# Products of a weight group in another order: all on the upper halves first, then those on the lower halves

## The chip, the cores and the metric

One core of a Trainium2 chip runs the whole program. The metric is the device time of one execution in microseconds. The engines are named as the profile names them: PE is TensorE (its weight loads are PEld), ACT is ScalarE, DVE is VectorE, POOL is GpSimd, SP is SyncE, which issues most of the DMAs.

## What is computed

Two blocks on 256 tokens of width 2048, in float32. The first is a mixer (attention and a state-space scan side by side) and a layer of product-key experts; the second is a pooling layer and an attention layer with an index that selects keys. All have large projections:

```python
def first_block(x, ...):
    h = x
    for layer in range(DEPTH):                  # DEPTH = 1
        xn = rms_norm(h, attn_norm[layer])
        h = h + hybrid_mixer(xn, w_in[layer], ..., w_out[layer])
        hn = rms_norm(h, ffn_norm[layer])
        h = h + peer_ffn(hn, peer_query[layer], peer_sub_keys[layer], peer_down[layer], peer_up[layer])
    return h

def second_block(x, c, ...):
    cond = jax.nn.silu(c)
    for i in range(DEPTH_2):                    # DEPTH_2 = 2
        mod = cond @ mod_w[i] + mod_b[i]
        shift, scale, gate = jnp.split(mod, 3, axis=-1)
        h = rms_norm_2(x, norm_g[i]) * (1.0 + scale[:, None, :]) + shift[:, None, :]
        ...                                     # pool_branch, then dsa_branch
        x = x + gate[:, None, :] * out
    return rms_norm_2(x, final_g)
```

## The kernel before

A float32 matrix product is made of three products of halves. Both operands are split into an upper half (the value rounded to the type float32r) and a lower half (the rest), and `mm3` adds x-lower by w-upper (L169), x-upper by w-lower (L170) and x-upper by w-upper (L171) into one accumulator in PSUM. The activations `x` are the stationary operand (128 x 128), the weights the moving one (128 x 512).

Weights come in groups of 1 MB: 4 blocks of 128 rows by 512 columns, in one tile `wr` of a pool of three. `split_w` issues the load on SP (L154) and makes the halves in two steps of two blocks each, into pools of three tiles `wh` and `wl`:

```python
wh = self.whp.tile([128, 2, 512], F32R, tag="wh", name=self.nm("wh"))
nc.scalar.activation(wh, wr[:, s], AF.Copy)                                    # L159, ACT
wl = self.wlp.tile([128, 2, 512], F32R, tag="wl", name=self.nm("wl"))
nc.vector.tensor_tensor(wl, wr[:, s], wh.bitcast(F32), op=OP.subtract)         # L161, DVE
```

So a group has two tiles `wh` and two tiles `wl`, here called the first and the second upper and lower half. `wl` needs `wh`, and the tile `wr` is free for another load once both `wl` of it are made. A new `wh` or `wl` needs the slot of the third last one, whose products must have run.

`product` (called by `linear`) runs the groups of a projection for 256 tokens: for each of the 4 blocks k and each of the 2 token tiles t the three products of `mm3`, 24 in a group. `product2` does it for the expert layer, where 192 of the tokens go through dense products: three products for the first 128 tokens into one accumulator, and two into another (L219 and L220), whose stationary tile `xp` holds the upper and the lower half of 64 tokens side by side; 20 in a group. The last 64 tokens of that layer take gathered rows of the expert tables instead (`gathers`: POOL issues the gathers at L772, DVE multiplies a row at L780 and adds one at L795, 2.3 us each). Gate values of the experts are read back from DRAM into tiles `fm` and multiplied at L865. With `skew`, the last two groups of a layer are drawn so that the first token tile ends early.

After each group `step` lets waiting pieces of other work (transposes, attention, the scan, parts of the modulation `mod_w` at L1014) follow in the program. The order on each engine is then set by a scheduler: instructions have the priority of their place in the code, the load and the split of weights stand 1000 places ahead (`PRIO`), and the scheduler takes what its own estimate of times says is ready. On the chip each engine runs its list in that order.

Of the kernel before, what the change touches and what calls it, by code (L numbers as in the profile page):

```python
# [37 lines left out]
class Kern:  # L38
# [139 lines left out]
    def product(self, ps, groups, first=True, last=True, hook=None, skew=False):  # L178


        n = len(groups)
        held = []
        for gi, (src, i, xs) in enumerate(groups):
            if hook:
                hook(gi)
            hs, ls = self.split_w(src, i)
            held += [(x, h, l, first and gi == kk == 0, last and gi == n - 1 and kk == 3)
                     for kk, (x, h, l) in enumerate(zip(xs, hs, ls))]
            m = 2 if skew and gi == n - 2 else len(held)
            now, held = held[:m], held[m:]  # L190
            order = [(a, t) for a in now for t in range(2)]
            if skew and gi == n - 1:
                order.sort(key=lambda a: a[1])
            for ((xh, xl), h, l, st, sp), t in order:
                s = slice(t * 128, t * 128 + 128)
                self.mm3(ps[t], xh[:, s], xl[:, s], h, l, st, sp)
            self.step()

    def product2(self, ps, groups, skew=False):

        n = len(groups)
        held = []
        mm = self.nc.tensor.matmul
        for gi, (src, i, xs) in enumerate(groups):
            hs, ls = self.split_w(src, i)
            held += [(x, h, l, gi == kk == 0, gi == n - 1 and kk == 3)
                     for kk, (x, h, l) in enumerate(zip(xs, hs, ls))]
            m = 2 if skew and gi == n - 2 else len(held)  # L210
            now, held = held[:m], held[m:]
            order = [(a, t) for a in now for t in range(2)]
            if skew and gi == n - 1:
                order.sort(key=lambda a: a[1])
            for ((xh, xl, xp), h, l, st, sp), t in order:
                if t == 0:
                    self.mm3(ps[0], xh, xl, h, l, st, sp)
                else:
                    mm(ps[1], xp, h, start=st, stop=False)  # L219
                    mm(ps[1], xp, l, start=False, stop=sp)  # L220
            self.step()

    def step(self):


        self.posts = [g for g in self.posts if next(g, self) is not self]
        while self.seq:
            if next(self.seq[0], self) is not self:
                break
            self.seq.pop(0)  # L230
        if self.pump:
            self.credit += PUMP
            while self.credit >= 1:
                self.credit -= 1
                next(self.pump, None)
        self.bg_due += self.bg_rate
        while self.bg_due >= 1:
            self.bg_due -= 1
            self.bg(1)
# [1263 lines left out]
```

## Time and profile before

| | |
|---|---|
| median of 3 runs | 2774.44 us (2774.32 to 2775.48) |
| the profiled execution, in all | 2777.65 us |
| its span from the first to the last instruction | 2775.9 us |
| its mean granted clock of TensorE | 0.983 |
| busy: PE, DVE, ACT | 2642.5, 2244.1, 1394.2 us |
| DMA | 782.08 MB, 282 GB/s in the mean |

Busy time is that of one profiled execution, on one core. A product of 128x512 counts as busy for about 0.39 us, but the next one issues before it ends, so that a busy PE isn't yet one that issues as often as it can; how far apart two products stand is read from their starts in the timeline. "[0.67 <-DVE wl L161]" behind a row is the idle time of the engine ahead of it, and what ended it. The chain is followed back from the last instruction, at each step to what released it.

### The profile page before, as it was taken

To read this page: it belongs to the slowest core of one execution; us is meant where nothing else is said; L and a number is where in the kernel's file an instruction comes from. 1 tells how busy PE (TensorE), PEld (TensorE's weight loads), DVE (VectorE), ACT (ScalarE), POOL (GpSimd) and SP (SyncE) were. 2 spreads that over 40 slices of the span, in tenths; PEclk is the share of its full clock that TensorE was granted. 3 is DMA by queue.
4 is the path that set the end of the run, shared out by engine and by line. 5 is a ranking of instruction groups with operands and counts; after the bars stand their busy time and mean duration, and the time that the engine had idled before them with its cause. 6 is when DMAs were issued, how large, how long until landed. Compare 5 with 4: busy or idle time off the path is not lost.

```text
span 2775.9 us, 33244 instructions
## 1 busy us (share of the span) xinstructions
PE 2642.5 (95%) x12296; PEld 2142.0 (77%) x12296; DVE 2244.1 (81%) x3162; ACT 1394.2 (50%) x1881; POOL 271.3 (10%) x210
## 2 busy tenths in 40 slices
PE   8999999998998999999999899998999799999998
PEld 6787778877876777787877677777887687888886
DVE  6988886999997898768998789967779867765655
ACT  5547555554654444454544444444444444455543
POOL 1000000001112222102322212000000000000000
PEclk9999999999999999999999999999999899999999
DMA  7666675557999999869999999765788855655554
GB/s 291 261 224 227 259 261 203 195 202 265 382 374 398 358 372 373 320 238 334 406 366 374 353 363 357 291 224 219 277 304 324 310 201 193 226 208 187 182 194 170
DMA packets 135123, 782.08 MB, mean 282 GB/s; under 512 B 14000, under 2 KB 38736, under 8 KB 43760
## 3 DMA queue, kind: packets, MB, share of 16 engines
q1 hardware_dynamic: 113680, 639.81, 62.4%
q0 software_dynamic: 20752, 138.53, 12.8%
q8 instruction: 96, 1.57, 0.2%
q10 hardware_dynamic: 528, 1.61, 0.2%
q14 instruction: 67, 0.55, 0.1%
HBM read 759.11 MB, written 20.23 MB: 281 GB/s over the span
## 4 chain that ended last, share of the span: by engine, by line
PE 64%; DVE 14%; DMA 13%; issue 4%; ACT 3%; POOL 0%; ACTq 0%; DVEq 0%; POOLq 0%; SPq 0%
PE acc L170 16%; PE acc L171 16%; PE acc L169 16%; DVE wl L161 6%; PE acc L219 5%; PE acc L220 5%; DMA wr<-in_down 4%; DMA wr<-in_up 4%; ACT wh L159 2%; DMA wr<-in_mod_w 2%; DVE md L1014 1%; PE tr L267 1%; DVE gl L795 1%; DVE fm L780 1%; DMA wr<-in_pool_w_out 1%
## 5 line engine op out<-in xcount | busy, mean ns | idle before, releaser
L159 ACT ACTIVATE wh<-wr 128x1024 fp32r<-128x1024 f32 x944 | 991.4, 1058 | 1127.1 <-PE acc L171 380.7
L161 DVE TENSOR_TENSOR wl<-wr,wh 128x1024 fp32r<-128x1024 f32 x944 | 1140.5, 1220 | 408.2 <-ACT wh L159 398.9
L170 PE MATMUL acc<-wl,fm 128*128 128x512 f32 x1952 | 775.0, 397 | 29.5 <-DVE wl L161 28.7
L169 PE MATMUL acc<-wh,fm 128*128 128x512 f32 x1952 | 780.6, 402 | 16.4 <-ACT wh L159 14.4
L171 PE MATMUL acc<-wh,fm 128*128 128x512 f32 x1952 | 768.3, 394 | 0.0
L170 PEld LDWEIGHTS acc<-wl,fm 128*128 128x128 f32 x1952 | 370.5, 190 | 124.1 <-DVE wl L161 50.7
L169 PEld LDWEIGHTS acc<-wh,fm 128*128 128x128 f32 x1952 | 369.5, 190 | 95.5 <-ACT wh L159 18.8
L171 PEld LDWEIGHTS acc<-wh,fm 128*128 128x128 f32 x1952 | 370.1, 190 | 75.0
L170 PE MATMUL acc<-wl,gl 128*128 128x512 f32 x768 | 307.9, 401 | 18.6 <-DVE wl L161 18.6
L169 PE MATMUL acc<-wh,gl 128*128 128x512 f32 x768 | 305.2, 398 | 10.6 <-ACT wh L159 9.4
L171 PE MATMUL acc<-wh,gl 128*128 128x512 f32 x768 | 302.6, 394 | 0.0
L1014 DVE SCALAR_TENSOR_TENSOR md<-wr,c_c,md 128x1024 f32<-128x1024 f32 x180 | 230.4, 1280 | 35.4 <-DMA wr<-in_mod_w 33.4
L219 PE MATMUL acc<-wh,s 128*128 128x512 f32 x512 | 202.8, 396 | 0.0
L220 PE MATMUL acc<-wl,s 128*128 128x512 f32 x512 | 202.7, 396 | 0.0
L219 PE MATMUL acc<-wh,fm 128*128 128x512 f32 x512 | 202.2, 395 | 0.0
L220 PE MATMUL acc<-wl,fm 128*128 128x512 f32 x512 | 202.0, 395 | 0.0
L170 PEld LDWEIGHTS acc<-wl,gl 128*128 128x128 f32 x768 | 145.2, 189 | 63.9 <-DVE wl L161 31.8
L169 PEld LDWEIGHTS acc<-wh,gl 128*128 128x128 f32 x768 | 145.0, 189 | 46.0 <-ACT wh L159 12.2
L772 POOL DMA_INDIRECT fm<-in_up_rows,slot_rows x64 | 124.0, 1938 | 482.1 <-DVE gl L795 257.0
L171 PEld LDWEIGHTS acc<-wh,gl 128*128 128x128 f32 x768 | 145.5, 189 | 31.7 <-issue 1.0
L795 DVE SCALAR_TENSOR_TENSOR gl<-fm,slot_act,gl 128x2048 f32<-128x2048 f32 x63 | 147.7, 2344 | 6.1 <-DMA fm<-in_up_rows,slot_rows 6.1
L780 DVE SCALAR_TENSOR_TENSOR fm<-fm,gl 128x2048 f32<-128x2048 f32 x64 | 146.1, 2284 | 0.2 <-DMA fm<-in_down_rows,slot_rows 0.2
(416 smaller groups left out, 2377.6 us busy)
## 6 DMA issues: line engine op xcount, KB each, us to landing
wr<-in_down SPq DMA_DIRECT2D x128, 1024.0 KB, 8.6
wr<-in_up SPq DMA_DIRECT2D x128, 1024.0 KB, 8.1
wr<-in_mod_w SPq DMA_DIRECT2D x96, 1024.0 KB, 5.2
wr<-in_attn_w_in SPq DMA_DIRECT2D x72, 1024.0 KB, 4.8
wr<-in_w_in SPq DMA_DIRECT2D x44, 1024.0 KB, 5.2
wr<-in_pool_w_in SPq DMA_DIRECT2D x32, 1024.0 KB, 5.3
wr<-in_w_out SPq DMA_DIRECT2D x16, 1024.0 KB, 4.8
wr<-in_peer_query SPq DMA_DIRECT2D x16, 1024.0 KB, 4.7
```

What stands on the lines that cost most here:

```text
L159: nc.scalar.activation(wh, wr[:, s], AF.Copy)
L161: nc.vector.tensor_tensor(wl, wr[:, s], wh.bitcast(F32), op=OP.subtract)
L169: mm(ps, xl, wh, start=first, stop=False)
L170: mm(ps, xh, wl, start=False, stop=False)
L171: mm(ps, xh, wh, start=False, stop=last)
L219: mm(ps[1], xp, h, start=st, stop=False)
L220: mm(ps[1], xp, l, start=False, stop=sp)
L267: self.nc.tensor.transpose(p[:, j, t * 128:(t + 1) * 128], src(t, k + j), self.ident)
L772: nc.gpsimd.indirect_dma_start(rows[j], None, d[src], bass.IndirectOffsetOnAxis(ap=ei[:, j:j + 1], axis=0))
L780: nc.vector.scalar_tensor_tensor(r, r, 1.0, x2, op0=OP.mult, op1=OP.mult, accum_out=act[:, j - 2:j - 1])
L795: nc.vector.scalar_tensor_tensor(acc, r, c, acc, op0=OP.mult, op1=OP.add)
L1014: nc.vector.scalar_tensor_tensor(acc, w[:, j], cd[:, k:k + 1], acc, op0=OP.mult, op1=OP.add)
```

## The change

Inside a group the products are put into another order. `product` and `product2` no longer call `mm3` or the matmul for each block and token tile, but write what there is to do into a list `todo`; the new function `halves` runs first all products of the list that read an upper half of the weights, and then all that read a lower half. Where the last group of a layer is drawn by token tile (`skew`), it does so for each token tile by itself. `split_w`, the pools and the number of products stay as they were.

```diff
+            todo = []
             for ((xh, xl), h, l, st, sp), t in order:
                 s = slice(t * 128, t * 128 + 128)
-                self.mm3(ps[t], xh[:, s], xl[:, s], h, l, st, sp)
+                todo.append((t, st, sp, [(xl[:, s], h), (xh[:, s], h)], [(xh[:, s], l)]))
+            self.halves(ps, todo, skew and gi == n - 1)
             self.step()
...
+            todo = []
             for ((xh, xl, xp), h, l, st, sp), t in order:
                 if t == 0:
-                    self.mm3(ps[0], xh, xl, h, l, st, sp)
+                    todo.append((t, st, sp, [(xl, h), (xh, h)], [(xh, l)]))
                 else:
-                    mm(ps[1], xp, h, start=st, stop=False)
-                    mm(ps[1], xp, l, start=False, stop=sp)
+                    todo.append((t, st, sp, [(xp, h)], [(xp, l)]))
+            self.halves(ps, todo, skew and gi == n - 1)
             self.step()
+
+    def halves(self, ps, todo, by_t):
+
+
+        for part in ([[a for a in todo if a[0] == t] for t in range(2)] if by_t else [todo]):
+            ops = [(t, st and i == 0, False, x, w) for t, st, _, up, _ in part for i, (x, w) in enumerate(up)]
+            ops += [(t, False, sp, x, w) for t, _, sp, _, low in part for x, w in low]
+            for t, st, sp, x, w in ops:
+                self.nc.tensor.matmul(ps[t], x, w, start=st, stop=sp)
```

On PE, in a group of `product2` in the stretch with gathers (it starts at 1077.92 us in the timeline of before), the first five products before; `acc_1753` and `acc_1754` are the two accumulators, `wh_1762` and `wl_1763` the first halves of the group, `wh_1764` and `wl_1765` the second, `fm_685` to `fm_687` the activations:

```order
L169 MATMUL acc_1753_9037<-wh_1762_9074,fm_686_3650 128x512 [waits Activation_49]
L170 MATMUL acc_1753_9037<-wl_1763_9076,fm_685_3649 128x512 [waits DVE_49]
L171 MATMUL acc_1753_9037<-wh_1762_9074,fm_685_3649 128x512
L219 MATMUL acc_1754_9038<-wh_1762_9074,fm_687_3651 128x512
L220 MATMUL acc_1754_9038<-wl_1763_9076,fm_687_3651 128x512
```

The tenth to the fourteenth product of the same group, changed:

```order
L232 MATMUL acc_1753_9037<-wh_1764_9078,fm_686_3650 128x512
L232 MATMUL acc_1753_9037<-wh_1764_9078,fm_685_3649 128x512
L232 MATMUL acc_1754_9038<-wh_1764_9078,fm_687_3651 128x512
L232 MATMUL acc_1753_9037<-wl_1763_9076,fm_685_3649 128x512 [waits DVE_49]
L232 MATMUL acc_1754_9038<-wl_1763_9076,fm_687_3651 128x512
```

The first product on `wl_1763`, and with it the wait for DVE, moved from the second place of the group to the thirteenth, behind all twelve products on `wh_1762` and `wh_1764`.

On DVE at the same place before (L780 is the product of a gathered row, L161 makes the lower halves):

```order
L161 TENSOR_TENSOR wl_1763_9076<-wr_1761_9072,wh_1762_9074 128x1024 [waits DMAHW4_49,Activation_49]
L780 SCALAR_TENSOR_TENSOR fm_1891_9743,slot_act_5650<-fm_1891_9743,gl_680_3640 128x2048 [waits DMASW0_49]
L161 TENSOR_TENSOR wl_1765_9080<-wr_1761_9072,wh_1764_9078 128x1024 [waits PE_49,Activation_49]
L161 TENSOR_TENSOR wl_1768_9106<-wr_1766_9102,wh_1767_9104 128x1024 [waits DMAHW5_49,PE_49,Activation_49]
L780 SCALAR_TENSOR_TENSOR fm_1909_9825,slot_act_5650<-fm_1909_9825,gl_680_3640 128x2048 [waits DMASW1_49]
```

And changed (L791 is the line that was L780, L901 adds an accumulator to `h`, L905 another to a sum):

```order
L791 SCALAR_TENSOR_TENSOR fm_1891_9743,slot_act_5650<-fm_1891_9743,gl_680_3640 128x2048 [waits DMASW0_49]
L161 TENSOR_TENSOR wl_1759_9047<-wr_1755_9039,wh_1758_9045 128x1024 [waits PE_49,Activation_49]
L161 TENSOR_TENSOR wl_1763_9076<-wr_1761_9072,wh_1762_9074 128x1024 [waits DMAHW4_49,PE_49,Activation_49]
L901 TENSOR_TENSOR h_118<-h_118,acc_1737_8956 128x512
L161 TENSOR_TENSOR wl_1765_9080<-wr_1761_9072,wh_1764_9078 128x1024 [waits PE_49,Activation_49]
L161 TENSOR_TENSOR wl_1768_9106<-wr_1766_9102,wh_1767_9104 128x1024 [waits DMAHW5_49,PE_49,Activation_49]
L905 TENSOR_TENSOR gl_1581_8164<-gl_1581_8164,acc_1738_8957 128x512
L791 SCALAR_TENSOR_TENSOR fm_1909_9825,slot_act_5650<-fm_1909_9825,gl_680_3640 128x2048 [waits DMASW1_49]
```

The gathered row that stood between `wl_1763` and `wl_1765` now stands two lower halves earlier, and the making of `wl_1763` waits for PE too.

On PE in the first layer, ahead of a group of `product` (`wh_120` is its first upper half, `tr_131` a block of transposes for the convolution), before:

```order
L267 MATMUL tr_131_892<-ident_104,s2_107_748 128x128
L267 MATMUL tr_131_892<-ident_104,s2_108_749 128x128
L169 MATMUL acc_117_813<-wh_120_817,fm_5_127 128x512 [waits Activation_49]
L169 MATMUL acc_118_814<-wh_120_817,fm_5_127 128x512
L170 MATMUL acc_117_813<-wl_121_819,fm_4_126 128x512 [waits DVE_49]
L171 MATMUL acc_117_813<-wh_120_817,fm_4_126 128x512
```

And changed (L278 is the line that was L267):

```order
L278 MATMUL tr_130_885<-ident_104,s2_107_748 128x128 [waits Activation_49]
L278 MATMUL tr_131_892<-ident_104,s2_107_748 128x128 [waits PE_49]
L232 MATMUL acc_117_813<-wh_120_817,fm_5_127 128x512 [waits Activation_49]
L232 MATMUL acc_117_813<-wh_120_817,fm_4_126 128x512
L232 MATMUL acc_118_814<-wh_120_817,fm_5_127 128x512
L232 MATMUL acc_118_814<-wh_120_817,fm_4_126 128x512
```

Most of the transposes moved behind the group, and the group begins with products on `wh_120` alone.

## Rows read from the trace of the kernel before

**Rows 1.** The page: busy time by engine, and the chain by engine.

```profile
PE 2642.5 (95%) x12296; PEld 2142.0 (77%) x12296; DVE 2244.1 (81%) x3162; ACT 1394.2 (50%) x1881; POOL 271.3 (10%) x210
...
PE 64%; DVE 14%; DMA 13%; issue 4%; ACT 3%; POOL 0%; ACTq 0%; DVEq 0%; POOLq 0%; SPq 0%
```

**Rows 2.** Waits, who for whom: us in total, times, longest us.

```profile
DVE wl L161 <- ACT wh L159: 398.9, 334, 11.2
ACT wh L159 <- PE acc L171: 380.7, 240, 4.5
...
PEld acc L170 <- DVE wl L161: 82.4, 89, 7.4
...
PE acc L170 <- DVE wl L161: 47.2, 57, 7.0
...
PEld acc L169 <- ACT wh L159: 31.0, 23, 9.2
```

**Rows 3.** The page's groups: busy us, mean ns, idle before, releaser.

```profile
L159 ACT ACTIVATE wh<-wr 128x1024 fp32r<-128x1024 f32 x944 | 991.4, 1058 | 1127.1 <-PE acc L171 380.7
L161 DVE TENSOR_TENSOR wl<-wr,wh 128x1024 fp32r<-128x1024 f32 x944 | 1140.5, 1220 | 408.2 <-ACT wh L159 398.9
```

**Rows 4.** Timeline, 1076 to 1086 us: start us, us, what, idle before.

```profile
1077.71 1.23 DVE L161 TENSOR_TENSOR wl<-wr,wh 128x1024 fp32r<-128x1024 f32 x1 [1.97 <-ACT wh L159]
...
1077.92 0.40 PE L169 MATMUL acc<-wh,fm 128*128 128x512 f32 x1
1078.85 2.28 DVE L780 SCALAR_TENSOR_TENSOR fm<-fm,gl 128x2048 f32<-128x2048 f32 x1
...
1078.99 0.50 PE L170 MATMUL acc<-wl,fm 128*128 128x512 f32 x1 [0.67 <-DVE wl L161]
...
1080.24 0.39 PE L170 MATMUL acc<-wl,fm 128*128 128x512 f32 x1
...
1080.26 2.00 ACT L159 ACTIVATE wh<-wr 128x1024 fp32r<-128x1024 f32 x2 [1.64 <-DMA wr<-in_down]
1080.47 0.39 PE L171 MATMUL acc<-wh,fm 128*128 128x512 f32 x1
...
1080.69 0.39 PE L219 MATMUL acc<-wh,fm 128*128 128x512 f32 x1
...
1081.06 2.35 DVE L161 TENSOR_TENSOR wl<-wr,wh 128x1024 fp32r<-128x1024 f32 x2
1081.15 0.39 PE L169 MATMUL acc<-wh,fm 128*128 128x512 f32 x1
...
1082.34 0.50 PE L170 MATMUL acc<-wl,fm 128*128 128x512 f32 x1 [0.80 <-DVE wl L161]
...
1084.28 0.39 PE L220 MATMUL acc<-wl,fm 128*128 128x512 f32 x1
```

**Rows 5.** The chain in order of time, three pieces: start us, us, what.

```profile
50.35 0.79 PE acc L170
...
998.03 0.03 DVEq L161
...
2192.57 0.50 PE acc L170
```

**Rows 6.** Stretches: us, busy by engine (instructions), clock, DMA share, GB/s.

```profile
694.00:1180.00 486.00, 454.95 (x2268) 363.36 (x2267) 423.21 (x431) 240.91 (x297) 100.00 (x61) 0.99 0.95 368
...
1250.00:1800.00 550.00, 523.66 (x2273) 417.97 (x2272) 492.61 (x443) 262.55 (x294) 118.98 (x64) 0.98 0.93 356
```

**Rows 7.** Timeline of DVE and of PE, 886 to 906 us.

```profile
901.46 0.96 DVE L865 TENSOR_TENSOR gl<-gl,fm 128x768 f32<-128x768 f32 x1 [7.87 <-DMA fm<-gates]
...
903.61 0.79 PE L170 MATMUL acc<-wl,fm 128*128 128x512 f32 x1 [6.97 <-DVE wl L161]
```

**Rows 8.** The page's DMA issues: times, KB each, us to landing.

```profile
wr<-in_down SPq DMA_DIRECT2D x128, 1024.0 KB, 8.6
wr<-in_up SPq DMA_DIRECT2D x128, 1024.0 KB, 8.1
```

More of the change, by code (lines that the diff above doesn't have):

```diff
@@ L204, in product2 @@
         held = []
-        mm = self.nc.tensor.matmul
         for gi, (src, i, xs) in enumerate(groups):
```

## The prediction, before the changed kernel ran

> **What bounds the kernel now.** I read the page's chain and busy shares first. TensorE is busy 95% of the span, and 64% of the chain that ended last lies on it [rows 1]; VectorE has 14% of the chain, DMA 13%. So most of the time is plain products, and the order of products takes nothing from those: their number stays. What an order can change is the rest of the chain, where TensorE waits. The table of waits says for what: the line that reads a lower half (L170) waited for the lower half (`wl`) for 47.2 us in 57 waits on PE, and the load ahead of it for 82.4 us in 89 waits; the load of the line that reads an upper half (L169) waited for it 31.0 us in 23 [rows 2]. The load's figure is the truer one, since a product stays "busy" for 0.39 us while the next could follow after 0.23 us. So the late operand is mostly the lower half. That is natural: ScalarE makes `wh` in 1058 ns, and only then VectorE makes `wl` from it in 1220 ns [rows 3].
>
> The timeline of one group shows it [rows 4]. The upper half is there and L169 issues at 1077.92; `wl` runs from 1077.71 for 1.23 us, so L170 issues only at 1078.99. VectorE then works 2.28 us on a gathered row (L780), the second `wl` comes after that at 1081.06, and L170 issues at 1082.34 where L169 had at 1081.15. The group's last product issues at 1084.28.
>
> Such a wait costs the span only where the chain goes through it. I counted in the chain's pieces: 32 times it enters TensorE at L170 behind a `wl`, first at 50.35, last at 2192.57 [rows 5]. Of these 22 lie between 694 and 1800 us, the two stretches with gathers, where DMA share is 0.95 and 0.93 and VectorE is busy 423 of 486 and 493 of 550 us [rows 6]: three resources are close to full there. The other 10 lie outside.
>
> **The change part by part.** Nothing is removed or added: as many products, loads, splits and DMAs. In a group of 20 products (a `product2` group) TensorE now runs 12 on upper halves and then 8 on lower ones; in a `product` group 16 and then 8. Products issue 0.227 us apart: L170 at 1080.24, L171 at 1080.47, L219 at 1080.69 [rows 4].
>
> *When operands are needed.* The first lower half was needed by the second product of a group (or third, where the scheduler drew an upper one forward); now by the 13th or 17th. That is 11 x 0.227 = 2.5 us of cover in the short group, against a lag of about 1.2 us. The second lower half was needed by product 12 and is now by product 17: 1.1 us more. The second upper half is needed earlier, by product 7 instead of 11; ScalarE makes both halves back to back (x2 in 2.00 us at 1080.26 [rows 4]), so it is 1.0 us behind the first and needed 1.36 us behind: covered. In the group at 1077.92 I get: 12 products to 1080.64, four on the first lower half (ready at 1078.94) to 1081.55, then a wait for the second until about 1082.34 as before, and the last product at 1083.02 instead of 1084.28: 1.26 us gained, though both waits were not removed in full.
>
> *The gain.* 82.4 us / 89 waits = 0.93 us for one; 32 on the chain: 29.8 us. One of them is 7 us long: VectorE stood 7.87 us behind a DMA of gate values, L170 then waited 6.97 us [rows 7]; there only 2.5 us are covered, so 4.5 us come off: **25.3 us**. Bounds: from 0 (every wait comes back as a wait for `wh`) to 82.4 us (all of them were worth something). The waits beside the chain I price at nothing: behind them TensorE would only have waited for the next DMA, and that is what is late next.
>
> *When buffers come free.* An upper half's slot is free earlier: after product 6 instead of 10 (the first), after 12 instead of 20 (the second). ScalarE now waits for TensorE at this point, 380.7 us behind L171 alone, and VectorE for ScalarE, 398.9 us in 334 waits [rows 2]. A lower half's slot is free later: the first after product 16 instead of 10. Before, `wl` of the next group could start at 10 x 0.227 + 1.06 (ScalarE first) = 3.33 us into a group, now at 16 x 0.227 = 3.63: 0.30 us later. For the other half it was 20 x 0.227 + 1.06, now it is 20 x 0.227: 1.06 us earlier. The chain leaves TensorE for VectorE's queue at L161 14 times (one at 998.03 [rows 5]), all in the gather stretches: between 14 x 0.30 = 4.2 us lost and 14 x 1.06 = 14.8 us gained. I take 0, since VectorE at 87 to 90% busy has little room to start earlier. Behind that `wl` on VectorE stand gathered rows of 2.28 us, sums of products and the release of the weight's DMA slot; with both halves alternating, that release moves by the same few tenths, against the 8.6 us that a load takes to land [rows 8].
>
> *Moved steps.* The scheduler puts some transposes of the first layer a group earlier or later among the products. A group is 24 x 0.227 = 5.4 us; I bound the effect by plus or minus one group and take 0.
>
> *A rule that speaks against it.* The loads: 12296 products stand beside 12296 loads [rows 1], and L171, which reads the same stationary slice as L170 ahead of it, issues 0.23 us after it, as L219 does with another slice [rows 4]. So sharing is worth nothing here. The Trainium skill (TensorE: Matmul & The Clock Gate, Part 2, step by step) says that loads are separate so that one can serve many products; by that the old order, with two products in a row on one stationary slice, should hold an advantage that the new one drops. The trace disagrees, and no row here prices such an advantage; were there one, it would show as another spacing, which is the last rival below.
>
> Sum: 2775.9 - 25.3 = 2750.6 us against the profiled span. That execution took 2777.65 us in all; the runs' median is 2774.44, so **2749 us**.
>
> **The rivals.**
>
> *DMA stays the bound in the gather stretches* (0.18). At a share of 0.95 and 0.93 an earlier product only waits longer for the next weights: the waits change names, from `wl` to `wh`. For it: TensorE's own waits for `wh` exist already [rows 2]. Against it: the chain runs on TensorE for long pieces between the DMA pieces, and the share isn't 1. Then only the 10 entries outside count: 10 x 0.93 = 9.3 us, less up to 4.2 us at the exits: 2765 to 2769 us. About half of this lies within 0.2% (5.5 us, which is about what a measurement of this kernel can tell from no change).
>
> *More comes back* (0.13). If the earlier upper slots let the queue of DMA, ScalarE and VectorE close its gaps, the gather stretches could shrink until DMA is full: 0.05 x 486 + 0.07 x 550 = 63 us: 2712 us at most, some 2725 if half of it and the outer 10 come.
>
> *VectorE's queue is blocked* (0.08, slower). `wl` for the first half now waits directly for TensorE, later in the group, and all behind it on VectorE waits too: the gathered rows, and the adds that free accumulators. The place is the 256 `product2` groups (128 loads of down, 128 of up [rows 8]). Price: 0.30 us each, 77 us if all pay; half of them, less the forecast's gain, is 38 - 25 = 13 us slower: 2787 us. It decides from the point where VectorE has under 0.30 us to spare in a group: now it has (486 - 423) / 486 = 13% of 4.5 us, 0.6 us, and 10%, 0.5 us, so it should hold. The row in which VectorE stood behind a gate DMA [rows 7] shows that such a block does reach TensorE. The Trainium skill (TensorE: Matmul & The Clock Gate, Part 1, on the array's architecture) calls ScalarE's and VectorE's queues strictly first in, first out; that row agrees.
>
> *The products themselves space differently* (0.03). One nanosecond on each of 12296 is 12.3 us. Now the spacing is the same where the accumulator changes and where it doesn't (L171 to L219, L170 to L171 [rows 4]), so I expect none.
>
> That the change doesn't do what it says is excluded by the rows of its order: upper ones first, lower ones behind.
>
> **How the numbers follow.** Forecast 0.58 (2749), more 0.13 (2712 to 2735), DMA-bound 0.18 (2765 to 2769), VectorE blocked 0.08 (2774 to 2826), spacing 0.03. Faster by over 0.2%: 0.58 + 0.13 + 0.08 = 0.79; within: 0.11; slower: 0.10. The range runs from 2716, near full DMA in the gather stretches, to 2772, which takes in the DMA-bound case; outside are the blocked VectorE and the last of "more".
>
> **What would show it.** Right: in the table of waits the products' wait for `wl` falls from 47.2 us to under 15; the chain enters TensorE at an upper half; products still 0.227 us apart; gather stretches some 17 us shorter. DMA-bound: the wait for `wh` grows by what `wl` lost and those stretches keep their length. Blocked: VectorE's `wl` waits for PE by tens of microseconds and the gathers' rows come later. Wrong altogether: another spacing, or new waits at transposes over 10 us.

## The result, and the profile after

The changed kernel took **2787.74 us** (median of 13 runs, 2777.35 to 2812.78) against 2774.32 us (13 runs, 2768.41 to 2782.84) for the kernel before on the same chip: a ratio of **1.0059, interval 1.0037 to 1.0081**. It is slower by about 0.6%, where 2749 us and "faster" had been forecast; the time lies outside the range, on the other side. The profiled execution took 2782.33 us, near the low end of its runs, so its trace shows about 5 us of a difference of 13.

The page of after, busy time by engine and the groups of the two halves (columns as in [rows 3]), answers [rows 1, 3]:

```profile
PE 2631.4 (95%) x12296; PEld 2139.7 (77%) x12296; DVE 2234.3 (80%) x3162; ACT 1392.1 (50%) x1881; POOL 284.3 (10%) x210
...
L159 ACT ACTIVATE wh<-wr 128x1024 fp32r<-128x1024 f32 x944 | 986.7, 1058 | 1078.1 <-PE acc L232 524.1
L161 DVE TENSOR_TENSOR wl<-wr,wh 128x1024 fp32r<-128x1024 f32 x944 | 1124.2, 1220 | 424.5 <-PE acc L232 274.4
...
wr<-in_down SPq DMA_DIRECT2D x128, 1024.0 KB, 6.9
wr<-in_up SPq DMA_DIRECT2D x128, 1024.0 KB, 7.3
```

The number of instructions and the mean time of each are the same. What is new is at the end of the second line: before, VectorE's idle time ahead of a lower half was for ScalarE (398.9 us); now most of it is for TensorE. The waits of after, who for whom, total, times and longest in us (all products of a group now stand on line 232), answer [rows 2]:

```profile
ACT wh L159 <- PE acc L232: 524.1, 415, 6.7
...
DVE wl L161 <- PE acc L232: 274.4, 147, 4.4
...
ACT wh L159 <- DMA wr<-in_up: 178.0, 66, 9.6
...
ACT wh L159 <- DMA wr<-in_down: 147.2, 58, 7.0
DVE wl L161 <- ACT wh L159: 143.8, 105, 6.4
...
PE acc L232 <- ACT wh L159: 41.2, 24, 9.9
PE acc L232 <- DVE wl L161: 34.5, 32, 2.9
```

The same view of before has for these:

```profile
ACT wh L159 <- DMA wr<-in_up: 113.4, 45, 12.3
ACT wh L159 <- DMA wr<-in_down: 109.2, 36, 7.6
...
PE acc L169 <- ACT wh L159: 23.8, 13, 9.2
...
DVE wl L161 <- PE acc L219: 4.9, 3, 2.5
...
DVE wl L161 <- PE acc L220: 1.4, 1, 1.4
```

Three things are to be seen. VectorE's wait for TensorE to let a lower slot go went from 6.3 us (4.9 and 1.4) to 274.4 us. ScalarE waited 103 us longer for the weights of down and up to land, 325.2 against 222.6, although a load landed sooner after its issue (6.9 and 7.3 us, against 8.6 and 8.1 in [rows 8]): so it went out later, as seen from ScalarE, which is itself free earlier now. And TensorE won 12.7 us on lower halves and lost 17.4 us on upper ones. The stretches with gathers answer [rows 6] (busy by engine, clock, DMA share, GB/s):

```profile
694.00:1180.00 486.00, 451.82 (x2224) 362.73 (x2224) 419.40 (x426) 238.14 (x293) 99.84 (x61) 0.98 0.94 364
1250.00:1800.00 550.00, 514.38 (x2228) 409.86 (x2227) 482.58 (x434) 254.46 (x289) 130.35 (x64) 0.99 0.92 353
```

Both hold fewer products (2224 and 2228 against 2268 and 2273) at fewer bytes a second (364 and 353 against 368 and 356): here the time was lost. Of VectorE's 274.4 us for TensorE only 20.5 lie in these two stretches (15.0 and 5.5 us in the same view of each). There the scheduler has drawn other operations ahead of the subtraction that would wait, so it shows as lateness. By the starts and ends of the instructions in the two stretches, the second subtraction of a weight tile began on the mean 1.2 and 1.4 us behind the end of its upper half in before, and 2.6 and 2.9 us in after. The tile itself, from the start of its first conversion to the end of its second subtraction, was in use for 5.5 and 5.7 us in before, and for 7.0 and 6.9 us in after. One group of after, with two of TensorE's rows, shows the way (timeline: start us, us, what, idle before):

```profile
978.96 2.01 ACT L159 ACTIVATE wh<-wr 128x1024 fp32r<-128x1024 f32 x2 [2.30 <-DMA wr<-in_up]
...
980.62 0.63 PE L232 MATMUL acc<-wh,s 128*128 128x512 f32 x1
...
981.05 0.63 PE L232 MATMUL acc<-wl,gl 128*128 128x512 f32 x1
...
982.54 1.23 DVE L161 TENSOR_TENSOR wl<-wr,wh 128x1024 fp32r<-128x1024 f32 x1 [1.24 <-PE acc L232]
...
983.80 0.33 SPq L154 DMA_DIRECT2D wr<-in_down  x1
```

Both upper halves of a tile are there at 980.97. Its second subtraction starts at 982.54, 1.57 us later, when TensorE is through with an earlier lower half. It ends at 983.77, and at 983.80 the next load goes out, 0.03 us behind it: the load waits for the weight tile that the subtraction still read. SyncE's own waits bear this out (SPq is its queue); in the first gather stretch of after the load (L154) waited 79 times for a lower half to be made (before: 79 times, 320.9 us):

```profile
SPq L154 <- DVE wl L161: 338.8, 79, 7.6
```

The size of the one wait above is no measure, though: TensorE's rows stand 0.43 us apart there in place of 0.227 (980.62, 981.05), since its granted clock was at the lower of its two levels, 0.50 of full speed, from 975 to 981 us. The means are over all tiles of the stretches.

### The profile page after: what moved, and what is told of

It reads as the page before. It is cut to its first block, busy times and chain, and to the rows that moved or that the text cites. A ratio compares the mean times of both kernels' runs of the same rounds, so it can differ in the third digit from the quotient of the medians.

```text
span 2780.6 us, 33436 instructions
## 1 busy us (share of the span) xinstructions
PE 2631.4 (95%) x12296; PEld 2139.7 (77%) x12296; DVE 2234.3 (80%) x3162; ACT 1392.1 (50%) x1881; POOL 284.3 (10%) x210
## 2 busy tenths in 40 slices
DMA packets 135124, 782.09 MB, mean 281 GB/s; under 512 B 14000, under 2 KB 38736, under 8 KB 43760
## 3 DMA queue, kind: packets, MB, share of 16 engines
q8 instruction: 96, 1.57, 0.2%
## 5 line engine op out<-in xcount | busy, mean ns | idle before, releaser
L161 DVE TENSOR_TENSOR wl<-wr,wh 128x1024 fp32r<-128x1024 f32 x944 | 1124.2, 1220 | 424.5 <-PE acc L232 274.4
L232 PE MATMUL acc<-wh,fm 128*128 128x512 f32 x4416 | 1096.1, 398 | 24.2 <-ACT wh L159 22.8
L232 PEld LDWEIGHTS acc<-wh,fm 128*128 128x128 f32 x4416 | 824.2, 190 | 201.2 <-ACT wh L159 29.0
L232 PE MATMUL acc<-wl,fm 128*128 128x512 f32 x2464 | 623.7, 393 | 13.2 <-DVE wl L161 12.7
L232 PEld LDWEIGHTS acc<-wl,fm 128*128 128x128 f32 x2464 | 459.8, 188 | 117.8 <-DVE wl L161 24.1
L232 PE MATMUL acc<-wh,gl 128*128 128x512 f32 x1536 | 449.4, 397 | 18.5 <-ACT wh L159 18.4
L232 PE MATMUL acc<-wl,gl 128*128 128x512 f32 x768 | 266.9, 396 | 21.8 <-DVE wl L161 21.7
L783 POOL DMA_INDIRECT fm<-in_up_rows,slot_rows x64 | 134.1, 2095 | 476.2 <-DVE gl L806 240.8
L791 DVE SCALAR_TENSOR_TENSOR fm<-fm,gl 128x2048 f32<-128x2048 f32 x64 | 146.1, 2284 | 0.0
L783 POOL DMA_INDIRECT fm<-in_down_rows,slot_rows x64 | 103.4, 1615 | 372.7 <-DVE fm L791 342.0
L232 PEld LDWEIGHTS acc<-wh,s 128*128 128x128 f32 x512 | 98.0, 191 | 23.8 <-DVE gl L905 2.0
L232 PEld LDWEIGHTS acc<-wl,s 128*128 128x128 f32 x512 | 96.5, 188 | 20.9 <-issue 0.5
L138 POOL TENSOR_TENSOR ri_y<-ri_v,mhalf 128x4 f32<-128x4 f32 (+2 forms) x18 | 17.4, 965 | 437.1 <-DVE ri_v L136 400.8
L278 PE MATMUL tr<-ident,s 128*128 128x128 f32 x296 | 45.2, 290 | 10.4 <-ACT s L1063 4.1
```

The costliest lines, as they stand in the source:

```text
L138: nc.gpsimd.tensor_tensor(y, v, self.mhalf.to_broadcast([128, n]), op=OP.pow)
L232: self.nc.tensor.matmul(ps[t], x, w, start=st, stop=sp)
L278: self.nc.tensor.transpose(p[:, j, t * 128:(t + 1) * 128], src(t, k + j), self.ident)
L783: nc.gpsimd.indirect_dma_start(rows[j], None, d[src], bass.IndirectOffsetOnAxis(ap=ei[:, j:j + 1], axis=0))
L791: nc.vector.scalar_tensor_tensor(r, r, 1.0, x2, op0=OP.mult, op1=OP.mult, accum_out=act[:, j - 2:j - 1])
```

## The experiments

All times are medians, with the kernel before run beside them (2775.1 to 2775.8 us in the four sets below); ratios are to that.

### One function at a time

e3 has the new order in `product` alone; e4 in `product2` alone.

```
e3, in product2:  mm3(ps[0], xh, xl, h, l, st, sp)      # as before
e4, in product:   mm3(ps[t], xh[:, s], xl[:, s], h, l, st, sp)   # as before
```

> The new order in product alone; product2, which runs in the stretches with gathers, as in the kernel before. The traces of before and changed have the new order 5 to 7 us ahead at 690 us and 12 to 15 us lost between 700 and 1750. Both theories: what is lost lies in product2, so 2764 to 2772 us. If it is the stages outside that lose: 2780 or more.

> The new order in product2 alone. Both theories: 2782 to 2796 us (the loss without the gain outside). If the loss needs product too: 2774.

e3: **2775.9 us, 1.0013 (0.9995 to 1.003)**: no difference. e4: **2786.88 us, 1.0046 (1.0027 to 1.0064)**, the changed kernel again. The loss is `product2`'s, the function of the gather stretches. The gain that was expected of `product` (2764 to 2772 us) isn't there, so e3's expectation missed. In the trace of before, TensorE's waits for a lower half are these in the first gather stretch, and then in the second:

```profile
PE acc L170 <- DVE wl L161: 24.9, 25, 7.0
```

```profile
PE acc L170 <- DVE wl L161: 18.4, 23, 2.4
```

That is 43.3 of the 47.2 us of [rows 2]. Outside these stretches there was next to nothing to win.

### The lower slots

e1 is the changed kernel with 2 slots for upper and 4 for lower halves, in the same memory; f1 is the kernel before with these pools.

```
-        self.whp = pool("wh", 3)
-        self.wlp = pool("wl", 3)
+        self.whp = pool("wh", 2)
+        self.wlp = pool("wl", 4)
```

> The changed kernel with the same memory dealt out otherwise: two tiles for upper halves, four for lower ones. Theory 1 (the lower halves' slots): a lower half now waits until product 16 of the group before last-but-one tile's readers, so it is made later behind its upper half (second tile 2.7 us behind instead of 1.4 in the gather stretch), the weight tile is held longer, and loads are issued later. With four slots that wait goes: VectorE's wait for PE at L161 falls from 274 us to under 60, the kernel comes to 2745 to 2768 us, below both. Theory 2 (DMA is full in the gather stretches, and the rest is the scheduler's order on VectorE): L161's wait for PE falls too, but the time stays at 2780 to 2795. Theory 3 (upper halves' slots matter more): two slots starve TensorE of upper halves, 2800 or more.

> The kernel before with 2 slots for upper and 4 for lower halves, the order of the products as it was; a control of e1 (2769.43 us). If the pools alone make e1's time, 2760 to 2770 us. If e1 owes it to the new order together with slots that fit it, the old order gains nothing from them, since its subtraction waited 4.9 us in all for TensorE to free a lower slot while ScalarE waited 668 us for an upper one: 2772 to 2800 us.

e1: **2769.43 us, 0.9974 (0.9957 to 0.9992)**, 18 us below the changed kernel, just above the expected 2745 to 2768, and under the one before. f1: **2894.97 us, 1.0416 (1.0397 to 1.0434)**. So the pools don't make e1's time: they cost the old order 120 us, more than expected, and give the new one 18. The waits of e1 show what went:

```profile
DVE wl L161 <- ACT wh L159: 376.7, 320, 5.5
...
ACT wh L159 <- DMA wr<-in_down: 101.6, 32, 7.4
ACT wh L159 <- DMA wr<-in_up: 74.5, 22, 7.4
```

VectorE's wait for TensorE to let a lower slot go has no row there any more; it waits for ScalarE as in before. ScalarE's wait for the loads is 176.1 us, against 325.2 in after. (That wait alone proves nothing: in e2, below, it is 328.0 us, and e2 is faster still.) The weight tile was in use for 4.6 and 4.8 us in the gather stretches, against 7.0 and 6.9 in after (counted as above). The late lower slot is thus the cause, whatever it acts through. Why it was late is plain from the count of slots. With three slots and two tiles to a group, the *second* lower half of a group needs the slot of the *first* of the group ahead. The new order reads that one up to its 16th product; the old one was done with it after the 10th.

### Shorter blocks

e2 runs the upper halves first inside each half of a group (two 128-row slices of the weight tile), h2 inside one slice of 128 rows; the order is the changed kernel's otherwise.

```
-  for part in (... if by_t else [todo]):
+  for part in (... if by_t else [todo[i:i + 4] for i in range(0, len(todo), 4)]):   # e2; 2 for 4 in h2
```

> Upper products first inside each half of a group only (six upper, four lower, six upper, four lower), so that slots of upper and lower halves come free after products 10 and 20 or sooner, as before, and the first lower half is still covered by six products (1.36 us). Theory 1: no longer hold of the weight tiles, most of the waits for lower halves gone: 2750 to 2768 us, L161's wait for PE under 60 us. Theory 2: 2775 to 2790.

> Both functions upper-first inside one 128-column slice of the weights alone (the two token tiles of one slice: 3 or 4 products with the upper half, then 2 with the lower), so the first product with a lower half comes fourth or fifth in its half tile and the lower slot is let go as before, one product from the end. If the gain of e2 grows with the products ahead of the first lower one, less of it is left here: 2762 to 2775 us. If what counts is that the lower slot is let go early, it is as good as e2 or better: 2745 to 2762 us.

e2: **2761.77 us, 0.9949 (0.9926 to 0.9971)**. h2: **2755.1 us, 0.992 (0.9899 to 0.9941)**, the fastest of all. Both beat the kernel before, and in both the weight tile was in use about as long as in before (5.6 and 5.9 us in e2, 5.6 and 5.5 in h2). h2 refutes the thought that the gain grows with the number of products ahead of the first lower one: in `product2` three ahead do as well as six, and better than twelve. Its waits:

```profile
PE acc L233 <- DVE wl L161: 28.8, 39, 2.5
...
PE acc L233 <- ACT wh L159: 26.7, 13, 9.9
...
DVE wl L161 <- PE acc L233: 3.5, 3, 1.9
```

The products' wait for a lower half fell further than in after (28.8 against 34.5 us), while the wait for an upper one stayed near before's 23.8, and VectorE's wait for TensorE is as small as before (3.5 us). The intervals of e2 and h2 overlap, so which of the two is better isn't settled.

h1 keeps the whole-group order in `product` and has e2's in `product2`; i4 has h2's there.

```
+  self.halves(ps, todo, skew and gi == n - 1, 99)   # product: the whole group
+  self.halves(ps, todo, skew and gi == n - 1, 4)    # product2: 4 in h1, 2 in i4
```

> product in the changed order over a whole group, product2 upper-first inside each half of a group alone (as in e2). If the loss is product2's whole-group order and nothing else, product may keep it: 2755 to 2766 us, as e2 (2761.77). If the whole-group order gains nothing in product (e3 was at 2775.9 us) and e2 had its gain there from the shorter blocks: 2766 to 2780 us.

> product in the changed order over a whole group, product2 upper-first inside one slice alone. If product is indifferent to the order (e3 was equal to the kernel before, h1 to e2), the time is h2's: 2750 to 2760 us. If the shorter block also gains in product: 2760 to 2772 us.

h1: **2761.77 us, 0.9959 (0.9944 to 0.9974)**; i4: **2758.74 us, 0.9937 (0.9911 to 0.9963)**. `product` is indifferent: in h1 VectorE waited 227.0 us for TensorE, all but 0.4 of it outside the gather stretches, and the time is e2's. The wait that the changed kernel shows most of costs nothing outside the gather stretches.

f2 puts e1's pools under e2's order.

> e2 (upper halves first inside each half of a group alone, 2761.77 us) with 2 slots for upper and 4 for lower halves. If what e1's pools cure is the late release of the lower slots, e2 has little of that left (VectorE waited 7.4 us for it in all) and the pools give it nothing: 2757 to 2770 us. If the pools help by themselves (loads let go earlier: first conversion to second subtraction 4.7 to 4.9 us in e1 against 5.7 to 6.0 in e2), 2745 to 2757 us.

f2: **2788.29 us, 1.0036 (1.0021 to 1.0051)**; both expectations were too low. e2 lets its second upper half go after product 16, e1 after 12, and I read the result as two upper slots being too few for that: the products' wait for `wh` is 52.2 us in f2, against 34.0 in e2. Slots must fit the order, and e2's order does better with three and three.

### VectorE's work on the gathered rows

f3 and f4 are the kernel before and the changed one with that work cut to 256 of 2048 columns; most of each gathered row is left out of the result.

```
-  nc.vector.scalar_tensor_tensor(r, r, 1.0, x2, ...)
+  nc.vector.scalar_tensor_tensor(r[:, 0:256], r[:, 0:256], 1.0, x2[:, 0:256], ...)
-  nc.vector.scalar_tensor_tensor(acc, r, c, acc, ...)
+  nc.vector.scalar_tensor_tensor(acc[:, 0:256], r[:, 0:256], c, acc[:, 0:256], ...)
```

> The kernel before, with VectorE's work on each gathered row tile cut from 2048 to 256 columns (the multiply with its sum, and the multiply-add; the gather transfers stay whole, so most of each row is left out of the result). It is the base of f4. The gather stretches are held by the transfers by the rows of before (DMA share 0.93 to 0.95), so either theory expects little from the cut alone: 2750 to 2780 us.

> The changed kernel with the same cut of VectorE's work on the gathered rows as f3; the number to read is f4 minus f3. Theory A (the weight tile is held 1.2 to 1.4 us longer because its second subtraction waits for the lower half's slot, so the next load is issued later, and the stretches that the transfers bound lose by that; the rows' work on VectorE is not needed for it): f4 is 5 to 20 us slower than f3. Theory B (the loss is made by the rows' work standing in VectorE's queue, ahead of or behind the subtraction that waits): without that work f4 is 5 to 25 us faster than f3.

f3: **2903.76 us, 1.0444 (1.0427 to 1.0462)**; f4: **2891.71 us, 1.0417 (1.04 to 1.0435)**. Less work made both some 4% slower, where 2750 to 2780 us had been expected of f3. In VectorE's order the operations on the rows stand on the mean 31 to 32 subtractions earlier in f3 than in before: the scheduler reckoned with shorter operations and drew them ahead, to where they wait for rows that haven't landed. Waits of f3:

```profile
DVE fm L780 <- DMA fm<-in_down_rows,slot_rows: 148.6, 36, 9.1
...
PE acc L170 <- DVE wl L161: 108.9, 59, 12.3
...
DVE gl L795 <- DMA fm<-in_up_rows,slot_rows: 94.5, 35, 8.5
```

243 us of waits for gathered rows stand against 6.3 in before, and the lower halves behind them are late. f4 is 12 us faster than f3, which is Theory B's sign; but the rows' hold on the queue grew rather than went away, so this pair doesn't tell the theories apart. It is **inconclusive** for its question.

### The gather transfers

g1 and g2 keep VectorE's operations whole and issue one gather in eight; eight operations in a row read the same tile, so seven eighths of the gathered rows are left out of the result.

```
+  if j % 8:
+      rows[j] = rows_of[0]
+      return
+  rows[j] = rows_of[0] = self.t_fm([128, D], F32)
```

> The kernel before with one gather transfer in eight: VectorE's 128 operations on gathered rows stay whole (2048 columns each), but eight of them in a row read the same tile, so seven eighths of the gathered rows are left out of the result. It is the base of g2. About 112 MB of the 782 MB go, and with them the DMA share of 0.93 to 0.95 in the gather stretches; of TensorE's 57 us of waits there a part goes: 2715 to 2765 us.

> The changed kernel with the same cut of the gather transfers as g1; the number to read is g2 minus g1. Theory A (the loss is made where transfers bound the stretch: the weight tile is held longer, so the next load is issued later and lands later): without that load on the DMA engines the order's own gain shows, g2 is 5 to 25 us faster than g1. Theory B (the loss is VectorE's time: it stands at 0.86 to 0.90 busy in these stretches with the rows' operations, and the wait for the lower slot uses up what is left): these operations are still there, so g2 is 5 to 15 us slower than g1.

g1: **2694.05 us** (2691.75 to 2694.48); g2: **2686.38 us** (2683.78 to 2691.93). Both lie below what was expected of g1 (2715 to 2765 us). The new order is 7.7 us *faster* here (five runs each; one of g2's lies among g1's), where it is 13.4 us slower with all the gathers: some 21 us depend on the transfers. VectorE's wait for the lower slot is as long as in after, and 50.6 us of it (28.0 and 22.6) lie in the gather stretches, where after had 20.5. The weight tile was in use for 7.4 and 7.0 us in these stretches, against 5.4 and 5.2 in g1. VectorE's row in g2, and g2's gather stretches:

```profile
DVE wl L161 <- PE acc L232: 287.6, 160, 6.0
```

```profile
694.00:1180.00 486.00, 485.76 (x2467) 400.46 (x2467) 449.31 (x459) 271.51 (x323) 10.39 (x6) 1.00 0.76 270
...
1250.00:1800.00 550.00, 542.35 (x2386) 441.10 (x2385) 510.22 (x487) 281.42 (x319) 18.51 (x11) 0.99 0.74 264
```

At a DMA share of 0.76 and 0.74 TensorE is busy for all but 8 us, and VectorE too is busier than in after (449 and 510 us). So VectorE's time isn't what limits, and neither its wait for the slot nor the longer use of the weight tile costs anything by itself. This is what Theory A expected: the late slot costs time where transfers bound the stretch, and not where they leave room.

### Which transfers

i1 (before), i2 (after) and i3 (h2) load each half of a weight tile into a slot of its own, six slots of half the size in place of three. The loads of `mod_w`, which take slots of the same pool, are halved too.

```
-  wr = self.wr.tile([128, 4, 512], ...);  nc.sync.dma_start(wr, wsrc[i])
+  for j in range(2):
+      wr = self.wr.tile([128, 2, 512], ...)
+      nc.sync.dma_start(wr, wsrc[i][:, j * 1024:(j + 1) * 1024])
```

> The kernel before with each weight load cut into two of 512 KB, each into its own half tile (6 slots of half the size in place of 3), so that a half is free as soon as its own subtraction is done. It is the base of i2. A load's first half can be let go some 1.2 to 2.5 us earlier, and there are twice as many issues: 2755 to 2785 us.

> The changed kernel with the same half loads; the number to read is i2 minus i1. Theory W (the weight loads carry the loss: the tile was held by the second subtraction, which waits for a lower slot): the first half's load no longer waits for it, so most of the loss is gone and i2 is equal to i1 or up to 20 us faster. Theory R (the gathered rows' transfers carry it, as their operations on VectorE and the slots that these free come later): cutting the weight loads changes nothing of that, i2 is 8 to 20 us slower than i1, as the changed kernel is against the one before.

> h2 (upper-first inside one slice, 2755.1 us) with half loads. If the weight loads' issue limits the gather stretches still: 2735 to 2752 us. If not, or if the doubled number of loads costs as much: 2752 to 2775 us.

i1: **2787.1 us, 1.0041 (1.0025 to 1.0057)**; i2: **2774.78 us, 0.999 (0.9973 to 1.0007)**; i3: **2779.03 us, 1.0009 (0.9992 to 1.0025)**. i1 and i3 lie above what was expected of them (2755 to 2785 and 2735 to 2775 us). In whole times, half loads cost the old order 11 us and h2 24 us, and give the changed kernel 13. But that price isn't paid in the gather stretches. There i1 ran more products than before in the first (2339 against 2268) and as many in the second; it fell back between 1800 and 2300 us. First i1, then before (columns as in [rows 6]):

```profile
694.00:1180.00 486.00, 467.94 (x2339) 375.56 (x2338) 433.48 (x442) 251.17 (x306) 102.68 (x61) 0.99 0.98 375
1250.00:1800.00 550.00, 523.74 (x2270) 419.26 (x2270) 492.57 (x445) 263.06 (x292) 134.76 (x64) 0.99 0.95 355
1800.00:2300.00 500.00, 458.01 (x2054) 367.07 (x2053) 376.14 (x510) 222.10 (x297) 11.14 (x21) 0.97 0.76 256
```

```profile
1800.00:2300.00 500.00, 476.39 (x2151) 383.46 (x2150) 390.14 (x523) 230.90 (x308) 11.13 (x21) 0.97 0.72 266
```

In this later stretch the loads of `mod_w` alternate with those of the pooling layer, and VectorE waited 66.1 us for them in i1, against 11.7 in before:

```profile
DVE md L1017 <- DMA wr<-in_mod_w: 66.1, 42, 4.0
```

```profile
DVE md L1014 <- DMA wr<-in_mod_w: 11.7, 7, 3.3
```

So the half loads are best read at the end of the gather stretches, by the start of the same conversion (the 621st of 944, at 1770 us in before). There i1 was 15 us ahead of before, i3 4 us ahead of h2, and i2 35 us ahead of after; between the two orders, i2 was 14 us ahead of i1, where after was 5.5 us behind before. These are single executions, good to several us. It is what Theory W expected: once the first half's load no longer waits for the second subtraction, the new order's loss is gone. And that subtraction is as late in i2 as in after, 2.5 us behind its upper half in both stretches (0.9 and 1.6 in i1), so the lateness alone isn't the loss. The old order gains as well, so its loads too had waited for their tile. The weight loads carry the loss, then, as far as such a pair can show it. That the gathered rows carry a part as well isn't excluded, but POOL's waits for the operations that free their slots hardly moved (327.5 and 257.0 us in before, 349.4 and 240.8 in after).

## Why the prediction was wrong

- **The gain, 25.3 us: mis-sized.** The mechanism is there. `wl` waits of TensorE fell from 47.2 to 34.5 us, the longest from 7.0 to 2.9; but "under 15" wasn't reached, 17.4 us came back as waits for `wh`, and where the transfers don't stand in the way the gain is 7.7 us (g1 to g2). The step took 0.93 us for each of 32 entries of the chain, although 22 of them lay where it had itself found three resources close to full.
- **"I take 0" for the slots: the step that failed.** Some 21 us were lost there. The prediction worked out 0.30 us lost on one lower half and up to 1.06 us gained on the other, and let them cancel. With three slots for two tiles the second of these doesn't exist: the first lower half of a group takes the slot of a half that was done with a whole group before, so nothing comes earlier. What remains is the loss, and it was more than 0.30 us: the second subtraction came 1.4 and 1.5 us later behind its upper half. It went to the release of the weight tile ("the same few tenths", which the step set against the 8.6 us of a landing and dropped); the tile was in use for 7.0 us in place of 5.5. At a DMA share of 0.95 part of such a late issue isn't made up, at 0.76 it is (g1, g2). Spread over the 256 groups of `product2`, 21 us would be 0.08 us for each; the runs don't show how they are spread.
- **The rival "VectorE's queue is blocked" (0.08)** had the function, the row (VectorE's `wl` waiting for PE by tens of microseconds) and, with 2787 us, the size. The size is luck: it is half of 77 us less a gain of 25, where the runs have some 21 less 7.7. Its mechanism wasn't the one either: VectorE wasn't short of time in g2, busier than in after, and half loads took the loss away with VectorE's work unchanged (i2). The time went through the loads that the weight tile lets go.
- **"DMA stays the bound" (0.18)** was right in that the waits changed names, 12.7 us off `wl` and 17.4 us onto `wh`. It had DMA only cap the gain; that the order could also lower what the transfers get done (368 to 364, 356 to 353 GB/s) wasn't seen.
- **Two slips on which nothing hangs.** "Some 2725" for *more comes back* should be 2734 (half of 63, and 9.3, off 2774.44). And the old order read the upper halves of a group up to products 9 and 19, not 10 and 20, which read lower ones.
- **Right:** the spacing of the products. Rows of after, TensorE at the change from upper to lower halves:

```profile
1437.39 0.39 PE L232 MATMUL acc<-wh,s 128*128 128x512 f32 x1
1437.62 0.39 PE L232 MATMUL acc<-wl,gl 128*128 128x512 f32 x1
1437.84 0.39 PE L232 MATMUL acc<-wl,s 128*128 128x512 f32 x1
```

- **The range:** its upper end, 2772, took in a rival in which the late slots cost 4.2 us at most. "77 us if all pay" stood in the same text as another rival's price, and a range that took it in would have held the 2787 us.

Open is why three products ahead of the first lower half do as well as six, how the 21 us divide between the single loads, and whether the gathered rows carry a part of them.

## What to carry to other kernels

When an order of reads is changed, write down for each operand which slot its successor takes (count modulo the number of slots), and from which instruction that slot is now free: holding an operand longer is paid by whoever loads behind it. Price that in the stretch where transfers are full, not on average: of VectorE's 274 us of waits the 254 outside the gather stretches cost nothing that the runs show, and the same late slot cost some 21 us inside them. And before going for the largest rearrangement, try the smallest that gives the operand its lead: three products ahead here, against twelve.

## What the runs showed of the hardware

- Loads cut from 1 MB to 512 KB, with the same bytes (216926 packets in place of 135123, 198256 of them under 8 KB in place of 43760), did not cost time in the stretch that is full of transfers: its DMA share rose from 0.95 to 0.98, for 375 in place of 368 GB/s, and it held 2339 products in place of 2268. They cost it between 1800 and 2300 us, at a share of 0.76 in place of 0.72 and 256 in place of 266 GB/s. The Trainium skill (DMA: Bandwidth & Descriptors, section Bandwidth) advises transfers of 1 MiB or more; these runs don't bear that out. The first stretch moved more with the halves, and in the later one the row that grew is VectorE's wait for `mod_w` (11.7 to 66.1 us), which can come from the order of the loads as well as from their size.
- In f3 the granted clock of the gather stretches fell to 0.92 and 0.95, where TensorE had 81 and 72 us of waits in them; in before it was 0.99 and 0.98 with 31 and 26 us:

```profile
694.00:1180.00 486.00, 404.73 (x1916) 322.03 (x1915) 262.66 (x377) 206.06 (x254) 82.22 (x58) 0.92 0.87 329
1250.00:1800.00 550.00, 477.50 (x2049) 380.68 (x2049) 337.08 (x390) 237.60 (x270) 91.28 (x64) 0.95 0.87 329
```

  f3's waits on TensorE sum to 96 us more than before's, its span is 127 us longer. The other 31 us are TensorE's busy time, 2673.6 us in place of 2642.5 for the same 12296 products. The lower clock goes with it; how much of the 31 us it made, and how much the waits (a product behind one counts as busy for 0.50 us in place of 0.39, [rows 4]), the rows don't tell.
- VectorE with 223 us less to do (2021.0 against 2244.1) made the kernel 128 us slower: where the instructions on the gathered rows stood in its queue (31 to 32 subtractions earlier) outweighed what they cost.
